# A two-layer float32 decoder trunk: streaming the high and low halves of the activations as one 512-column product

## The chip, the cores and the metric

The kernel runs on one core of one Trainium2 chip. The metric is the device time of one execution in microseconds, as the median over repeated runs of the same program; lower is better. Besides these times there is one execution that was recorded by the hardware profiler, and every row shown below comes from that execution. Engines are named as the profile names them: PE is the matrix engine, PEld its weight loads, DVE the vector engine, ACT the scalar engine, POOL the GpSimd engine, SP the queue that issues the loads.

## The reference, cut to what matters

Two layers (`DEPTH = 2`) over 256 positions and a width of 1024. Each layer computes

```python
h = rmsnorm(x, norm1[l]); proj = h @ w_in[l]
hq, hf, hi, hg, aq, ak, av, ga, gb = split_cols(proj)
...                                   # gated recurrence on hq, hf, hi, hg -> y_a
...                                   # sliding-window attention on aq, ak, av -> y_b
x = x + (sigmoid(ga) * y_a + sigmoid(gb) * y_b) @ w_o[l]
h2 = rmsnorm(x, norm2[l])
x = x + (silu(h2 @ w_gate[l]) * (h2 @ w_up[l])) @ w_down[l]
```

and a final rmsnorm follows. All of it is float32. The hidden width of the feed-forward part is 2816, that is 22 blocks of 128.

## The kernel before

**Products in three terms.** A float32 product is made from three products in the faster type `float32r`: each operand is split into a high half (the value rounded to `float32r`) and a low half (what the rounding left), and high·high, high·low and low·high are added up in PSUM; low·low is left out. Weights are split as they arrive: ACT casts a *unit* of 128 x 1024 weights to its high half `wh`, and DVE subtracts to get the low half `wl` (`ahead`, lines 192 to 203). There are 300 units. A unit waits for one of five buffers (`NW = 5`), which comes free when PE has used the unit that was in it; the raw weights lie in three buffers of 1 MB (`NRAW = 3`) that SP fills. `take(n)` (line 205) hands out the next units and asks for the following ones; `used()` (line 211) counts a finished unit and asks for the unit four further on.

**Activations.** `Norm` (line 272) transposes x, multiplies it by the gain and splits it into the two tiles `xh` and `xl`, each [128, 8, 256]: eight blocks `k` of the width by 256 positions. There is one buffer of each.

**Two forms of the product.** In `form_a` (line 222) the activations are the stationary operand and 512 columns of weights stream: each product is 128 x 512. It serves most projections, and `down` (line 848) does the same with `mm3`. In `form_b` (line 249) a 128 x 128 block of weights is the stationary operand and the 256 positions stream, so that the result comes out transposed. One unit is eight values of `k` with three products of 256 columns each, 24 in all, into half of a PSUM bank (a bank holds 512 float32 values per partition). `form_b` serves

- the 16 units of hf and hq per layer (`pb`, lines 713 to 721), while the generator of the attention is advanced beside them,
- the 22 units of the gate (`pg`) and the 22 of the up projection (`pu`) per layer, in `gate_up` (line 812), which takes two units of each at a time: eleven calls per layer, sorted into six groups (the last of one call).

In `gate_up`, DVE multiplies the whole bank `pg` by the row factors `rb2` into `z`, ACT takes the sigmoid into `sgm`, DVE multiplies the two, then multiplies `z` by the bank `pu`; `split` (line 259) makes the halves `ah` and `al`. `down` uses them one group later: group `gi - 1` follows the `gate_up` calls of group `gi`, and after the last group the last two are done together.

**PSUM.** There are eight banks: four with the tag `mm`, which turn over among all projections, two `at` and two `hg`. During the feed-forward part `at` and `hg` hold the four sums of `down` (`acc`).

**Order.** Generators are advanced by `run` (line 352): at each `yield` of the main line of products, the side generators (attention, recurrence, norms) may issue their next piece. A scheduler then orders the instructions of each engine by this order and by when they are ready by its own reckoning; each engine executes its own list strictly in order.

Of the kernel before, what the change touches and what calls it, by code (L numbers as in the profile page):

```python
# [8 lines left out]
F32R = mybir.dt.float32r  # L9
# [3 lines left out]
ALU = mybir.AluOpType  # L13
AX = mybir.AxisListType

P = 128
D = 1024
S = 256
NT = S // P
DEPTH = 2  # L20
KT = D // P
# [19 lines left out]
def trunk(ctx, tc, x, norm1, w_in, lb_logits, hg_norm, attn_sinks, w_pa, w_pb, w_o, norm2,  # L41
# [4 lines left out]
    class Ordered:  # L46
        def __init__(self, engine):
            self.engine = engine
            self.always = engine is nc.tensor
# [10 lines left out]
    V, A, G, T = (Ordered(e) for e in (nc.vector, nc.scalar, nc.gpsimd, nc.tensor))  # L60

    hp = ctx.enter_context(tc.tile_pool(name="hp", bufs=1))
    hp.tile([P, 224], F32, tag="lead", name="lead")
    hp.tile([P, KT, S], F32R, tag="xh", name="xh_lead")
    hp.tile([P, KT, S], F32R, tag="xl", name="xl_lead")
    st = hp.tile([P, 8, P], F32, tag="st", name="st")
    cp = ctx.enter_context(tc.tile_pool(name="cp", bufs=1))
    rawp = ctx.enter_context(tc.tile_pool(name="rawp", bufs=NRAW))
# [5 lines left out]
    def psum(name, tag="mm"):  # L74
        return pp.tile([P, 512], F32, tag=tag, name=name, bufs=4 if tag == "mm" else 2)

    def btile(shape, name, tag="b", dt=F32):
        return big.tile(shape, dt, tag=tag, name=name, bufs=6)

    def ztile(shape, name, tag="z", dt=F32):  # L80
        return sm.tile(shape, dt, tag=tag, name=name, bufs={"z": 4, "hx": 4, "rp": 2}[tag])
# [110 lines left out]
    def ahead(n):  # L192
        while len(ready) < min(n, 2 * len(plan)):
            while loaded[0] < len(plan) and len(raws) < len(ready) + 4:
                load(loaded[0])
                loaded[0] += 1
            i = len(ready)
            shape = list(raws[i].shape)
            hi = wp.tile(shape, F32R, tag="wh", name=f"wh{i}")
            lo = wp.tile(shape, F32R, tag="wl", name=f"wl{i}")  # L200
            A.copy(hi, raws[i])
            V.tensor_tensor(lo, raws[i], hi.bitcast(F32), ALU.subtract)
            ready.append((hi, lo))

    def take(n):
        i = taken[0]
        ahead(i + max(n, NW - 1))
        taken[0] += n
        return ready[i:i + n]

    def used():
        done[0] += 1
        ahead(done[0] + NW - 1)
# [32 lines left out]
                    used()  # L246
                yield

    def form_b(ps, act, unit, ks=range(KT)):
        wh, wl = unit  # L250
        for k in ks:
            (ah, al), kk = act(k)
            T.matmul(ps, wh[:, k, :], ah[:, kk, :], start=k == 0, stop=False)
            T.matmul(ps, wh[:, k, :], al[:, kk, :], start=False, stop=False)
            T.matmul(ps, wl[:, k, :], ah[:, kk, :], start=False, stop=k == KT - 1)
            if k % 4 == 3:
                yield

    def split(hi, lo, src):
        A.copy(hi, src)  # L260
        V.tensor_tensor(lo, src, hi.bitcast(F32), ALU.subtract)
# [10 lines left out]
    class Norm:  # L272
        def __init__(self, gain, name):
            self.gain, self.name = gain, name
            self.xh = hp.tile([P, KT, S], F32R, tag="xh", name=f"xh_{name}")
            self.xl = hp.tile([P, KT, S], F32R, tag="xl", name=f"xl_{name}")
            self.rb = sm.tile([P, 1, S], F32, tag="rb", name=f"rb_{name}", bufs=1)
            self.ss = sm.tile([P, NT, 3], F32, tag="ss", name=f"ss_{name}")
            self.r = [sm.tile([P, 1], F32, tag=f"r{t}", name=f"r_{name}{t}") for t in range(NT)]

        def act(self, k):
            return (self.xh, self.xl), k
# [53 lines left out]
    def start(gen, wait=0):  # L336
        sides.append([gen, wait])
        return sides[-1]
# [9 lines left out]
    def finish(side):  # L348
        while side[0] is not None:
            step(side)  # L350
# [8 lines left out]
    def layer(l, n1):  # L359
        act, rs, rb, spread = n1.act, n1.r, n1.wide(), n1.spread  # L360
# [327 lines left out]
        def recurrence():  # L688
            while atd[0] is not None:
                yield 1  # L690
            for g in range(2):
                decays(g)
            yield YD
            for g in range(2):
                yield from scores(g)
                yield 2
                yield from outputs(g)
# [15 lines left out]
        for g in range(2):  # L713
            for dst in fqk[g][:2]:
                for b in range(2):
                    ps = psum(f"pb{l}{g}{b}").rearrange("p (a c) -> p a c", a=2)
                    units = take(2)
                    for i in range(2):
                        yield from form_b(ps[:, i, :], act, units[i])
                        used()  # L720
                    V.tensor_tensor(dst[:, 2 * b:2 * b + 2], ps, rb, ALU.mult)
        rec = start(recurrence(), 1)

        def put_gate(c):
# [59 lines left out]
        n2 = Norm(g2[:, l], f"n2_{l}")  # L784
# [21 lines left out]

        for p_ in parts:
            finish(p_)
        act2, rs2, rb2, spread2 = n2.act, n2.r, n2.wide(), n2.spread
        acc = [[psum(f"acc{l}{t}{c}", "at" if t == 0 else "hg") for c in range(2)] for t in range(NT)]  # L810

        def gate_up(gi, b, ah, al):
            first = gi == 0 and b == 0
            pg = psum(f"pg{l}{gi}{b}").rearrange("p (a c) -> p a c", a=2)
            pu = psum(f"pu{l}{gi}{b}").rearrange("p (a c) -> p a c", a=2)
            z = ztile([P, 2, S], f"zg{l}{gi}{b}")
            sgm = ztile([P, 2, S], f"sgm{l}{gi}{b}")

            def mid():
                V.tensor_tensor(z, pg, rb2, ALU.mult)  # L820
                A.activation(sgm, z, AF.Sigmoid)
                V.tensor_tensor(z, z, sgm, ALU.mult)

            units = take(4)
            if first:
                for ks in (range(KT // 2), range(KT // 2, KT)):
                    yield from form_b(pg[:, 0, :], act2, units[0], ks)
                    yield from form_b(pu[:, 0, :], act2, units[2], ks)
                spread2()
                yield from form_b(pg[:, 1, :], act2, units[1])  # L830
                mid()
                used()
                used()
                yield from form_b(pu[:, 1, :], act2, units[3])
                used()
                used()
            else:
                for i in range(2):
                    yield from form_b(pg[:, i, :], act2, units[i])
                    used()  # L840
                mid()
                for i in range(2):
                    yield from form_b(pu[:, i, :], act2, units[2 + i])
                    used()
            V.tensor_tensor(z, pu, z, ALU.mult)
            split(ah[:, 2 * b:2 * b + 2], al[:, 2 * b:2 * b + 2], z)

        def down(item, ts_, c, units, tell):
# [14 lines left out]
        for gi, (b0, nb) in enumerate(groups):  # L863
            ah = btile([P, 4, S], f"ah{l}{gi}", "r", F32R)
            al = btile([P, 4, S], f"al{l}{gi}", "r", F32R)
            for b in range(nb // 2):
                yield from gate_up(gi, b, ah, al)
            pend.append((b0, nb, ah, al))
            if gi and gi < len(groups) - 1:
                item = pend.pop(0)  # L870
                for c in range(2):
                    yield from down(item, range(NT), c, take(2), True)
# [65 lines left out]
    for l in range(DEPTH):  # L938
        hold = []

        def whole():
            hold.append((yield from layer(l, nx)))

        run(whole())
        nx = hold[0]
# [53 lines left out]
```

## Time and profile before

| | |
|---|---|
| median of 3 runs | 957.61 us (957.34 to 957.65) |
| profiled execution, its own time | 957.52 us |
| span of that execution, first to last instruction | 955.8 us |
| mean granted clock of PE, as a share of full speed | 0.998 |
| instructions | 16173 |
| moved by DMA | 161.24 MB, mean 169 GB/s |

The span is what the rows can explain; 1.7 us of the profiled execution's own time lie around it. A group row gives the number of instructions, their summed busy time, the mean of one, and the idle time of the engine just ahead of them. The mean of one matmul runs from its start to its modelled end, and neighbours overlap: the distance between starts is shorter than that mean. The chain rows divide the time without overlap.

### The profile page before, as it was taken

What the parts mean: (1) busy time and instruction counts of PE and PEld (TensorE: products, weight loads), DVE (VectorE), ACT (ScalarE), POOL (GpSimd) and SP (SyncE); (2) the same over time, 40 slices, a digit from 0 to 9 for tenths busy, and PEclk for the clock granted to TensorE, in tenths of its full rate; (3) what the DMA queues carried; (4) which work ended last, traced back from release to release, by engine and by line L of the source; (5) the groups of instructions that cost most, each with busy time, mean ns of one, the idle gap of its engine ahead of it and who ended that gap; (6) DMA issues with size and microseconds to landing.
All of it is one profiled execution on the core that took longest, in us unless ns stands there. A gap on an engine that the chain in (4) does not pass through costs nothing.

```text
span 955.8 us, 16173 instructions
## 1 busy us (share of the span) xinstructions
PE 940.6 (98%) x6666; PEld 830.2 (87%) x6666; DVE 639.3 (67%) x1056; ACT 502.6 (53%) x794; POOL 16.4 (2%) x28
## 2 busy tenths in 40 slices
PE   7999999999999999999999999999999999999996
PEld 5879997878889999999878899878788899999995
DVE  6566769976677656555575676798857766556554
ACT  6555595545445444444365765855454544444442
POOL 1000000000000000000000000000000000000000
PEclk9999999999999999999999999999999999999999
DMA  8635444544445555555465334554545565555531
GB/s 283 225 129 172 148 157 140 170 135 173 149 162 180 186 203 182 176 184 195 151 207 190 132 133 138 172 178 133 161 159 180 162 197 177 177 190 190 193 133 44
DMA packets 110937, 161.24 MB, mean 169 GB/s; under 512 B 2768, under 2 KB 64400, under 8 KB 110864
## 3 DMA queue, kind: packets, MB, share of 16 engines
q1 hardware_dynamic: 110160, 159.12, 51.2%
q8 instruction: 52, 0.85, 0.4%
q10 hardware_dynamic: 704, 1.10, 0.3%
q14 instruction: 21, 0.17, 0.0%
HBM read 159.15 MB, written 1.05 MB: 168 GB/s over the span
## 4 chain that ended last, share of the span: by engine, by line
PE 96%; ACT 1%; DMA 1%; DVE 1%; issue 0%; POOL 0%; POOLq 0%; ACTq 0%
PE pg L55 13%; PE pu L55 13%; PE acc L55 12%; PE pb L55 10%; PE yb L55 5%; PE ga L55 5%; PE gb L55 5%; PE gate L55 5%; PE ya L55 5%; PE wo L55 5%; PE aq L55 5%; PE v L55 4%; PE akv L55 2%; PE qk L55 1%; PE pv L55 1%; PE o L55 1%
## 5 line engine op out<-in xcount | busy, mean ns | idle before, releaser
L55 ACT CAST wh<-raw 128x1024 fp32r<-128x1024 f32 x300 | 314.1, 1048 | 356.8 <-PE pg L55 71.8
L55 DVE TENSOR_TENSOR wl<-raw,wh 128x1024 fp32r<-128x1024 f32 x300 | 366.4, 1224 | 198.5 <-ACT wh L55 196.3
L55 PE MATMUL pg<-xh_n,wh 128*128 128x256 f32 x352 | 99.9, 284 | 0.0
L55 PE MATMUL pu<-xh_n,wh 128*128 128x256 f32 x352 | 99.9, 284 | 0.0
L55 PE MATMUL pg<-xl_n,wh 128*128 128x256 f32 x352 | 99.8, 284 | 0.0
L55 PE MATMUL pu<-xl_n,wh 128*128 128x256 f32 x352 | 99.8, 283 | 0.0
L55 PE MATMUL pu<-xh_n,wl 128*128 128x256 f32 x352 | 99.8, 283 | 0.0
L55 PE MATMUL pg<-xh_n,wl 128*128 128x256 f32 x352 | 99.7, 283 | 0.0
L55 PE MATMUL pb<-xh_n,wh 128*128 128x256 f32 x256 | 74.5, 291 | 0.0
L55 PE MATMUL pb<-xh_n,wl 128*128 128x256 f32 x256 | 72.7, 284 | 0.0
L55 PE MATMUL pb<-xl_n,wh 128*128 128x256 f32 x256 | 72.5, 283 | 0.0
L55 PE MATMUL acc<-wl,ah 128*128 128x512 f32 x176 | 68.9, 392 | 0.0
L55 PE MATMUL acc<-wh,al 128*128 128x512 f32 x176 | 68.6, 390 | 0.0
L55 PE MATMUL acc<-wh,ah 128*128 128x512 f32 x176 | 68.4, 392 | 0.0
L55 PEld LDWEIGHTS pg<-xl_n,wh 128*128 128x128 f32 x352 | 67.6, 192 | 0.4
L55 PEld LDWEIGHTS pg<-xh_n,wh 128*128 128x128 f32 x352 | 67.6, 192 | 0.4
L55 PEld LDWEIGHTS pu<-xh_n,wl 128*128 128x128 f32 x352 | 67.7, 192 | 0.0
L55 PEld LDWEIGHTS pu<-xl_n,wh 128*128 128x128 f32 x352 | 67.7, 192 | 0.0
L55 PEld LDWEIGHTS pu<-xh_n,wh 128*128 128x128 f32 x352 | 67.6, 192 | 0.0
L55 PEld LDWEIGHTS pg<-xh_n,wl 128*128 128x128 f32 x352 | 67.6, 192 | 0.0
L55 PEld LDWEIGHTS pb<-xh_n,wh 128*128 128x128 f32 x256 | 49.1, 192 | 3.0 <-issue 3.0
L55 PEld LDWEIGHTS pb<-xl_n,wh 128*128 128x128 f32 x256 | 49.2, 192 | 0.0
(232 smaller groups left out, 1856.2 us busy)
## 6 DMA issues: line engine op xcount, KB each, us to landing
raw<-in_w_in SPq DMA_DIRECT2D x58, 1024.0 KB, 5.1
raw<-in_w_gate SPq DMA_DIRECT2D x22, 1024.0 KB, 5.2
raw<-in_w_up SPq DMA_DIRECT2D x22, 1024.0 KB, 5.2
raw<-in_w_down SPq DMA_DIRECT2D x22, 1024.0 KB, 5.0
raw<-in_w_pb SPq DMA_DIRECT2D x8, 1024.0 KB, 5.0
raw<-in_w_pa SPq DMA_DIRECT2D x8, 1024.0 KB, 5.2
raw<-in_w_o SPq DMA_DIRECT2D x8, 1024.0 KB, 5.0
raw<-in_w_in SPq DMA_DIRECT2D x4, 512.0 KB, 6.2
```

The costliest lines, as they stand in the source:

```text
L55: ins = call(*args, **kw)
```

## The change

`xh` and `xl` become the two halves of one tile `xx` of shape [128, 8, 2, 256], so that for each `k` the high and the low half lie side by side as 512 columns. `form_b` then makes one product of `wh` with all 512 columns and one of `wl` with the 256 high columns: two products for each `k` instead of three. The result fills a whole bank, with the part from the low halves in its right half. A new function `join` adds the two halves: ACT copies the right half to SBUF and DVE adds the left half to it. Every unit has a bank of its own, and the operations that read `pg`, `pu` and `pb` from PSUM read the joined values from SBUF. The diff, cut to its core:

```diff
-    hp.tile([P, KT, S], F32R, tag="xh", name="xh_lead")
-    hp.tile([P, KT, S], F32R, tag="xl", name="xl_lead")
+    hp.tile([P, KT, 2, S], F32R, tag="xx", name="xx_lead")
...
-    def form_b(ps, act, unit, ks=range(KT)):
+    def form_b(ps, n, unit, ks=range(KT)):
         wh, wl = unit
         for k in ks:
-            (ah, al), kk = act(k)
-            T.matmul(ps, wh[:, k, :], ah[:, kk, :], start=k == 0, stop=False)
-            T.matmul(ps, wh[:, k, :], al[:, kk, :], start=False, stop=False)
-            T.matmul(ps, wl[:, k, :], ah[:, kk, :], start=False, stop=k == KT - 1)
+            if k < KT - 1:
+                T.matmul(ps, wh[:, k, :], n.xx[:, k], start=k == 0, stop=False)
+            T.matmul(ps[:, 0:S], wl[:, k, :], n.xx[:, k, 0, :], start=False, stop=False)
+            if k == KT - 1:
+                T.matmul(ps, wh[:, k, :], n.xx[:, k], start=False, stop=True)
             if k % 4 == 3:
                 yield
+
+    def join(dst, ps):
+        A.copy(dst, ps[:, S:])
+        V.tensor_tensor(dst, ps[:, 0:S], dst, ALU.add)
...
-                    ps = psum(f"pb{l}{g}{b}").rearrange("p (a c) -> p a c", a=2)
                     units = take(2)
                     for i in range(2):
-                        yield from form_b(ps[:, i, :], act, units[i])
+                        ps = psum(f"pb{l}{g}{b}{i}")
+                        yield from form_b(ps, n1, units[i])
+                        join(dst[:, 2 * b + i], ps)
                         used()
-                    V.tensor_tensor(dst[:, 2 * b:2 * b + 2], ps, rb, ALU.mult)
+                    V.tensor_tensor(dst[:, 2 * b:2 * b + 2], dst[:, 2 * b:2 * b + 2], rb, ALU.mult)
...
-            pg = psum(f"pg{l}{gi}{b}").rearrange("p (a c) -> p a c", a=2)
-            pu = psum(f"pu{l}{gi}{b}").rearrange("p (a c) -> p a c", a=2)
+            pg = [psum(f"pg{l}{gi}{b}{i}") for i in range(2)]
+            pu = [psum(f"pu{l}{gi}{b}{i}") for i in range(2)]
...
-                V.tensor_tensor(z, pg, rb2, ALU.mult)
+                V.tensor_tensor(z, z, rb2, ALU.mult)
...
                 for i in range(2):
-                    yield from form_b(pg[:, i, :], act2, units[i])
+                    yield from form_b(pg[i], n2, units[i])
+                    join(z[:, i], pg[i])
                     used()
                 mid()
                 for i in range(2):
-                    yield from form_b(pu[:, i, :], act2, units[2 + i])
+                    yield from form_b(pu[i], n2, units[2 + i])
+                    join(sgm[:, i], pu[i])
                     used()
-            V.tensor_tensor(z, pu, z, ALU.mult)
+            V.tensor_tensor(z, z, sgm, ALU.mult)
```

The first call of `gate_up` in a layer, which works on two units in turn, is changed in the same way.

## Rows read from the trace of the kernel before

**Rows 1.** The page: busy time of the engines, and the last chain by engine

```profile
PE 940.6 (98%) x6666; PEld 830.2 (87%) x6666; DVE 639.3 (67%) x1056; ACT 502.6 (53%) x794; POOL 16.4 (2%) x28
...
PE 96%; ACT 1%; DMA 1%; DVE 1%; issue 0%; POOL 0%; POOLq 0%; ACTq 0%
```

**Rows 2.** The chain that ended last, in order of time: start us, us, what

```profile
94.64 5.95 PE pb L55 x48
...
146.54 11.15 PE gate L55 x48
...
200.89 5.49 PE yb L55 x24
...
338.27 10.91 PE acc L55 x48
349.18 5.75 PE pg L55 x48
354.93 5.76 PE pu L55 x48
360.69 5.76 PE pg L55 x48
```

**Rows 3.** Groups, shapes kept apart, PE: form B products, then one of 512 columns

```profile
L55 PE MATMUL pg<-xl_n,wh 128*128 128x256 f32 x352 | 99.8, 284 | 0.0
L55 PE MATMUL pu<-xl_n,wh 128*128 128x256 f32 x352 | 99.8, 283 | 0.0
...
L55 PE MATMUL pb<-xl_n,wh 128*128 128x256 f32 x256 | 72.5, 283 | 0.0
...
L55 PE MATMUL acc<-wh,al 128*128 128x512 f32 x176 | 68.6, 390 | 0.0
```

**Rows 4.** Groups, shapes kept apart, ACT and DVE

```profile
L55 ACT CAST wh<-raw 128x1024 fp32r<-128x1024 f32 x300 | 314.1, 1048 | 356.8 <-PE pg L55 71.8 <-PE acc L55 68.3 <-PE pu L55 63.4
...
L55 ACT COPY rb_n<-rp_n 128x256 f32<-128x256 f32 x4 | 1.5, 366 | 1.7 <-PE rp_n L55 1.7
...
L55 DVE TENSOR_TENSOR wl<-raw,wh 128x1024 fp32r<-128x1024 f32 x300 | 366.4, 1224 | 198.5 <-ACT wh L55 196.3
L55 DVE TENSOR_TENSOR zg<-pg,rb_n 128x512 f32<-128x512 f32 x22 | 15.2, 692 | 15.1 <-PE pg L55 15.1
L55 DVE TENSOR_TENSOR zg<-zg,sgm 128x512 f32<-128x512 f32 x22 | 15.1, 686 | 0.0
...
L55 DVE TENSOR_TENSOR att1l<-pv,att1h 128x256 fp32r<-128x256 f32 x8 | 3.1, 420 | 0.7 <-ACT att1h L55 0.7
```

**Rows 5.** Stretches: from:to and length, busy us and count per engine, PEclk, DMA share, GB/s

```profile
0.00:16.00 16.00, 9.31 (x33) 6.99 (x34) 8.40 (x13) 8.85 (x15) 2.62 (x11) 1.00 0.85 303
...
90.00:128.00 38.00, 38.00 (x331) 36.20 (x329) 25.87 (x77) 23.07 (x54) 0.00 (x0) 1.00 0.38 119
128.00:158.00 30.00, 30.00 (x168) 25.21 (x165) 24.60 (x31) 23.80 (x35) 0.00 (x0) 1.00 0.53 173
...
338.00:372.00 34.00, 34.00 (x243) 32.11 (x242) 19.88 (x20) 14.68 (x16) 0.00 (x0) 1.00 0.56 186
```

**Rows 6.** Timeline of ACT in one call of gate_up

```profile
351.97 1.05 ACT L55 CAST wh<-raw 128x1024 fp32r<-128x1024 f32 x1 [1.66 <-PE pg L55]
354.85 1.05 ACT L55 CAST wh<-raw 128x1024 fp32r<-128x1024 f32 x1 [1.83 <-PE pg L55]
```

**Rows 7.** Timeline of DVE in the first call of gate_up of layer 0

```profile
295.17 0.69 DVE L55 TENSOR_TENSOR xl_n<-xg_n,xh_n 128x512 fp32r<-128x512 f32 x1 [0.42 <-ACT xh_n L55]
```

**Rows 8.** Timeline at the end of layer 0: ACT, then DVE

```profile
470.81 1.06 ACT L55 CAST wh<-raw 128x1024 fp32r<-128x1024 f32 x1 [6.77 <-PE acc L55]
...
464.70 0.68 DVE L55 TENSOR_TENSOR al<-zg,ah 128x512 fp32r<-128x512 f32 x1
```

More of the change, by code (lines that the diff above doesn't have):

```diff
@@ L274, in __init__ @@
             self.gain, self.name = gain, name
-            self.xh = hp.tile([P, KT, S], F32R, tag="xh", name=f"xh_{name}")
-            self.xl = hp.tile([P, KT, S], F32R, tag="xl", name=f"xl_{name}")
+            self.xx = hp.tile([P, KT, 2, S], F32R, tag="xx", name=f"xx_{name}")
+            self.xh, self.xl = self.xx[:, :, 0, :], self.xx[:, :, 1, :]
             self.rb = sm.tile([P, 1, S], F32, tag="rb", name=f"rb_{name}", bufs=1)
@@ L808, in layer @@
             finish(p_)
-        act2, rs2, rb2, spread2 = n2.act, n2.r, n2.wide(), n2.spread
+        rs2, rb2, spread2 = n2.r, n2.wide(), n2.spread
         acc = [[psum(f"acc{l}{t}{c}", "at" if t == 0 else "hg") for c in range(2)] for t in range(NT)]
@@ L826, in gate_up @@
                 for ks in (range(KT // 2), range(KT // 2, KT)):
-                    yield from form_b(pg[:, 0, :], act2, units[0], ks)
-                    yield from form_b(pu[:, 0, :], act2, units[2], ks)
+                    yield from form_b(pg[0], n2, units[0], ks)
+                    yield from form_b(pu[0], n2, units[2], ks)
+                join(z[:, 0], pg[0])
                 spread2()
-                yield from form_b(pg[:, 1, :], act2, units[1])
+                yield from form_b(pg[1], n2, units[1])
+                join(z[:, 1], pg[1])
                 mid()
+                join(sgm[:, 0], pu[0])
                 used()
                 used()
-                yield from form_b(pu[:, 1, :], act2, units[3])
+                yield from form_b(pu[1], n2, units[3])
+                join(sgm[:, 1], pu[1])
                 used()
```

## The prediction

> **What bounds the kernel now.** I read the page first. PE is busy for 98% of the span, and the chain that ended last is PE for 96% of it [rows 1]; DVE (67%) and ACT (53%) have room. So a saving of PE time shows up in the time, and work added to DVE and ACT shows up only where PE then waits for it. The granted clock is 1.00, the 2.4 GHz level, in every stretch I looked at [rows 5], and nothing here gives PE a pause that would change it.
>
> The next question is what one product costs PE. The groups say 284 ns for 256 columns and 390 ns for 512 [rows 3]. Taken at their word, 960 replaced pairs (352 of pg, 352 of pu, 256 of pb) would save 2 x 284 - 390 = 178 ns each. But these means overlap: a start is not a whole mean after the one before. The chain in order of time divides the time without overlap, and there 48 products of 256 columns take 5.75 to 5.76 us, 120.0 ns each, and 48 of 512 columns take 10.91 us, 227.3 ns each [rows 2]. The 256 further columns cost 107.3 ns, 0.42 ns a column, which is one column per cycle at 2.4 GHz. What is left, 120.0 - 107.3 = 12.7 ns, is the fixed part of one product with its weight load. The reader should see here that the stream of columns is nearly everything: the change streams exactly as many columns as before (512 + 256 against 3 x 256 for each k) and saves one fixed part.
>
> **The change part by part.**
>
> *Products.* Each k goes from three products to two, from 3 x 120.0 = 360.0 ns to 227.3 + 120.0 = 347.3 ns. There are 960 values of k [rows 3], and all of them lie on the chain: 960 x 12.7 = 12.2 us. A unit goes from 24 x 120.0 = 2.88 us to 8 x 347.3 = 2.78 us. No row shows a 512-column product with this stationary operand, so I bound the price by other 512-column rows: 228.8 ns (24 of yb in 5.49 us) and 232.3 ns (48 of gate in 11.15 us, the beginning of a stage in it) [rows 2], which leave 11.2 and 7.7 ns per pair, 10.8 and 7.4 us. From above, if the whole fixed part of both products went, it would be 2 x 12.7 x 960 = 24 us, but the acc row still has a fixed part with 512 columns, so I keep 12.2. I take the acc row because it stands directly beside pg and pu and nothing is mixed into it.
>
> A rule speaks against this saving. The rows show a fixed part of 12.7 ns. The Trainium skill ("TensorE: Matmul & The Clock Gate", section "Back-to-back issue gap") gives N/2.4 + 2.5 ns for warm products, so a fixed part of only 2.5 ns; by that the sum would be about 2.4 us, an estimate from that page. The trace does not agree: 256 columns would then take 109 ns, and they take 120.0.
>
> *The joins.* Each of the 120 form B units (16 + 44 per layer) adds an ACT copy of 128 x 256 from PSUM, 0.37 us as rb_n, and a DVE addition of 128 x 256 with one operand in PSUM, 0.42 us as att1l [rows 4]. That is 44 us more on ACT and 50 us more on DVE. The multiplications by rb stay and read SBUF instead of PSUM: 0.69 us either way [rows 4], so no change. If all the joins stood on the path, it would be 120 x 0.79 = 95 us; if they are hidden, nothing. They are near nothing, for these reasons:
>
> - In a steady stretch of the feed-forward part DVE is busy 19.88 of 34 us and ACT 14.68 [rows 5]. A period holds eight form B units, so DVE goes to 23.2 and ACT to 17.6 of some 33.2 us, 70% and 53%.
> - PE does not read z, sgm or pu. The halves ah and al are read by down one group later, behind at least the next 10.91 us of acc. At the end of a layer al is ready at 465.4 us, and the last weights that the last down needs are only cast from 470.81 on [rows 8]: a join of 0.79 us fits in.
> - Queue order: the join's copy on ACT waits for the end of its unit, and behind it stands the cast of a coming unit. Casts now start at the end of a unit, when its buffer comes free [rows 6], and serve the unit five further on. Held up by one unit plus the copy, the halves are ready 0.37 + 1.05 + 1.22 = 2.6 us after a unit's end, with three units of 2.78 us, 8.3 us, to go. Slack 5.7 us. DVE's subtraction stands behind the addition in the same way.
> - PSUM: one call of gate_up now takes all four mm banks instead of two. A bank is cleared some 0.9 us after its unit and wanted again three units later, 8.3 us.
> - SP: nothing is moved past it. Its loads start when a cast and a subtraction free a raw buffer, so a little later in each round; the stretch moves 186 GB/s at a share of 0.56 where the opening stretch moved 303 [rows 5], so a rate higher by 1% is covered.
>
> *One tile for both halves.* A 512-column product needs the low half at once, where until now its high half could go first. This can matter only where PE stands right behind the split: the first gate_up of a layer, where xl takes 0.69 us after xh [rows 7]. Bound: 0 to 0.7 us in each of two layers. Since the first calls also hold k's and units that are ready earlier, I take 0.15 us each, 0.3 us in all. In the pb stretch and behind it, where ACT is busy 23.80 and DVE 24.60 of 30 us [rows 5], a late cast could cost something; the 5.7 us of slack cover it, and I put 0 there with up to 3 us kept for the range (about eight copies, 8 x 0.37 us, laid fully on the path).
>
> *Sum.* 957.52 - 12.2 + 0.3 = 945.6 us against the profiled execution. The median of the runs shown is 0.1 us higher, so 945.7.
>
> **The rivals.**
>
> *The fixed part is smaller than it looks (no change).* If most of the 12.7 ns belonged to the conditions of the 256-column stages and came back with 512 columns and these weights, say as in a row at 237.5 ns, the pair would give 2.5 ns: 2.4 us, 955.2 us. Against it: four kinds of 512-column rows lie at 227 to 232 ns. The skill's rule above leads to about this time. Chance 0.05, and the losses of the next rival, if they ate most of the gain, lead there too, 0.03.
>
> *Part of the gain is given back.* The added 94 us on ACT and DVE reorder their lists; around the end of pb both are near full [rows 5], and side work of the attention and the recurrence shares them. Three to eight microseconds of PE waits would leave 949 to 953.5. For: 48 products of pb already take 5.95 instead of 5.76 us [rows 2], so that stage is less smooth. Against: PE has no idle time there now. Chance 0.14.
>
> *Slower: PE waits for PSUM banks.* With all four mm banks in one call of gate_up, the next unit's first product must wait for the join if the banks do not turn over in time. It decides from the point where a bank is wanted before its DVE addition is done. The price is up to copy plus addition, 0.79 us a unit, 95 us, 1040 us; the kernel comes out slower by over 0.2% once a unit loses (12.2 + 1.9)/120 = 0.12 us. For: half as many blocks fit into the banks as before. Against: three other units lie between. Chance 0.05.
>
> *The means of the groups are right after all.* 960 x 178 ns = 171 us, 787 us. Against it: 24 products at 284 ns would take 6.8 us a unit and two units take 5.76. Also smaller windfalls, down to twice the fixed part (24 us, 933 us), go here. Chance 0.03.
>
> **How the numbers follow.** The forecast, 945.7 us, has a chance of 0.70, from 943.5 (fixed parts a little larger, nothing lost) to 948.9 (the gate row's price of a product, and some loss). The range has to hold 8 in 10, so it goes on into the rival of the given-back gain up to 951. A measurement of this kernel can tell about 0.2%, 1.9 us, from no change. Faster: 0.70 + 0.14 + 0.03 and about half of the 0.08 of the first rival, since 955.2 lies just beyond the limit, 0.91; within 0.2%: 0.04; slower: 0.05.
>
> **What would show it.** In the changed profile: 960 fewer PE instructions (6666 to 5706) and as many fewer weight loads; in the chain in order of time, two form B units in about 5.56 us, so a gate-and-up call of 11.1 us against 11.5; acc unchanged at 10.91 us for 48. ACT about 547 us busy and DVE about 690. Casts that still wait for PE, not PE for casts. Wrong would be: pairs of a 512- and a 256-column product that take 355 ns or more (the fixed part), products that wait for a DVE addition (banks), or idle time of PE behind ACT's casts.

## The result, and the profile after

The changed kernel takes 951.12 us (median, 950.94 to 951.57) against 957.61 us: a ratio of 0.9934 with a 95% interval of 0.9916 to 0.9951. The sign and the bounding engine came out as forecast, the size did not: 6.5 us were saved where 11.9 were expected, and the time lies 0.1 us above the range.

The page of the changed kernel shows what the change was meant to do, beside [rows 1]:

```profile
span 949.5 us, 14350 instructions
...
PE 934.3 (98%) x5706; PEld 778.0 (82%) x5706; DVE 678.5 (71%) x1176; ACT 538.4 (57%) x914; POOL 16.5 (2%) x28
...
PE 95%; DVE 2%; ACT 2%; DMA 0%; issue 0%; POOL 0%; POOLq 0%; ACTq 0%; SPq 0%
```

There are 960 products and 960 weight loads fewer, and 120 instructions more on each of DVE and ACT. PE is still what ends last. The chain in order of time (start us, us, what), which answers to [rows 2], shows where the gain stayed small:

```profile
336.81 10.88 PE acc L55 x48
347.69 5.63 PE pg L55 x32
353.33 5.64 PE pu L55 x32
358.97 5.64 PE pg L55 x32
```

Two units take 5.64 us, not the 5.56 us forecast: 5.64 us / 16 = 352.5 ns for each k instead of 347.3. The acc stage beside it has not become dearer (10.88 us for 48, 226.7 ns each). PE's timeline (start us, us, engine, line, operation) shows that nothing is waited for; the products simply stand further apart than in the stages that the price came from:

```profile
348.22 0.40 PE L55 MATMUL pg<-xx_n,wh 128*128 128x512 f32 x1
348.46 0.28 PE L55 MATMUL pg<-xx_n,wl 128*128 128x256 f32 x1
348.58 0.40 PE L55 MATMUL pg<-xx_n,wh 128*128 128x512 f32 x1
348.82 0.28 PE L55 MATMUL pg<-xx_n,wl 128*128 128x256 f32 x1
348.93 0.40 PE L55 MATMUL pg<-xx_n,wh 128*128 128x512 f32 x1
```

Read the starts, not the lengths: from a 512-column product to the next start it is 0.24 us, where acc has 0.227; from a 256-column one 0.12 and 0.11. Over the whole gate-and-up part the mean distance is 235.1 ns after a 512-column product (700 of them) and 117.7 ns after one of 256 (704). All means of this kind below are worked out from the starts in the record of the same part, leaving out distances over 260 ns, which stand beside other products (the transposes and the attention's) or hold a wait.

The joins are where they were expected to be. Groups of the changed kernel, which answer to [rows 4]:

```profile
L55 ACT COPY zg<-pg 128x256 f32<-128x256 f32 x44 | 16.4, 373 | 57.2 <-PE pg L55 57.2
...
L55 DVE TENSOR_TENSOR zg<-pg,zg 128x256 f32<-128x256 f32 x44 | 18.7, 424 | 23.0 <-ACT zg L55 22.9
L55 DVE TENSOR_TENSOR sgm<-pu,sgm 128x256 f32<-128x256 f32 x44 | 18.4, 421 | 11.1 <-ACT sgm L55 11.1
```

0.37 us on ACT and 0.42 us on DVE, as taken from rb_n and att1l; over all four kinds (zg, sgm, q, f) the copies add up to 43.9 us and the additions to 50.4, as forecast. That the page has ACT at 538.4 and DVE at 678.5 us, not at the 547 and 690 forecast, is because neighbouring records overlap, and the page counts the time that two of them share once: DVE's single durations add up to 742.8 us, 48.7 more than before. And a stretch of the feed-forward part, columns as in [rows 5]:

```profile
338.00:372.00 34.00, 34.00 (x180) 29.09 (x179) 23.24 (x30) 17.58 (x26) 0.00 (x0) 1.00 0.60 188
```

DVE 23.24 and ACT 17.58 of 34 us (forecast 23.2 and 17.6), PE without a pause, its granted clock at 1.00.

### The profile page after: what moved, and what is told of

The parts are those of the page before. It is cut to its first block, busy times and chain, and to the rows that moved or that the text cites. A ratio compares the mean times of both kernels' runs of the same rounds, so it can differ in the third digit from the quotient of the medians.

```text
span 949.5 us, 14350 instructions
## 1 busy us (share of the span) xinstructions
PE 934.3 (98%) x5706; PEld 778.0 (82%) x5706; DVE 678.5 (71%) x1176; ACT 538.4 (57%) x914; POOL 16.5 (2%) x28
## 4 chain that ended last, share of the span: by engine, by line
PE 95%; DVE 2%; ACT 2%; DMA 0%; issue 0%; POOL 0%; POOLq 0%; ACTq 0%; SPq 0%
PE pg L55 13%; PE pu L55 13%; PE acc L55 12%; PE pb L55 9%; PE yb L55 5%; PE ga L55 5%; PE gb L55 5%; PE gate L55 5%; PE wo L55 5%; PE ya L55 5%; PE aq L55 5%; PE v L55 4%; PE akv L55 2%; PE qk L55 1%; PE o L55 1%; PE pv L55 1%
## 5 line engine op out<-in xcount | busy, mean ns | idle before, releaser
L55 PE MATMUL pu<-xx_n,wh 128*128 128x512 f32 x352 | 125.1, 398 | 0.0
L55 PE MATMUL pg<-xx_n,wh 128*128 128x512 f32 x352 | 125.0, 398 | 0.0
L55 PE MATMUL pu<-xx_n,wl 128*128 128x256 f32 x352 | 91.8, 281 | 0.0
L55 PE MATMUL pg<-xx_n,wl 128*128 128x256 f32 x352 | 91.6, 281 | 0.0
L55 PE MATMUL pb<-xx_n,wh 128*128 128x512 f32 x256 | 91.3, 403 | 0.0
L55 PEld LDWEIGHTS pg<-xx_n,wh 128*128 128x128 f32 x352 | 64.8, 188 | 12.4
L55 PEld LDWEIGHTS pu<-xx_n,wh 128*128 128x128 f32 x352 | 64.8, 188 | 11.9
L55 PEld LDWEIGHTS pu<-xx_n,wl 128*128 128x128 f32 x352 | 66.5, 189 | 4.0
L55 PEld LDWEIGHTS pg<-xx_n,wl 128*128 128x128 f32 x352 | 66.5, 189 | 4.0
L55 PE MATMUL pb<-xx_n,wl 128*128 128x256 f32 x256 | 66.9, 281 | 0.0
```

The costliest lines, as they stand in the source:

```text
L55: ins = call(*args, **kw)
```

## The experiments

The first theory (A) was that right after a change of size PE's products stand further apart and come back only after some ten of the same size, as the starts of the acc stage suggest. Its rivals: (B) the joins slow PE, (C) a 512-column stream of these activations is slower by itself.

**Eight of one size in a row.** The products of the changed kernel in another order:

```diff
-        for k in ks:
-            if k < KT - 1:
-                T.matmul(ps, wh[:, k, :], n.xx[:, k], start=k == 0, stop=False)
-            T.matmul(ps[:, 0:S], wl[:, k, :], n.xx[:, k, 0, :], start=False, stop=False)
...
+        if ks[0] == 0:
+            T.matmul(ps, wh[:, 0, :], n.xx[:, 0], start=True, stop=False)
+        for k in ks:
+            T.matmul(ps[:, 0:S], wl[:, k, :], n.xx[:, k, 0, :], start=False, stop=False)
+        if len(ks) == KT:
+            yield
+        for k in ks:
+            if k:
+                T.matmul(ps, wh[:, k, :], n.xx[:, k], start=False, stop=k == KT - 1)
+        yield
```

The last unit's seven and the next unit's first 512-column product make eight.

> Only the order of the products in a form B unit changes: runs of eight of one size (eight 512-column products, then eight of 256) instead of alternating sizes. Theory A (settling: right after a change of size a 512-column product starts 230 to 241 ns before the next, and comes down to 227 ns after some ten of the same size; alternating sizes never settle): eight 512-column products at 234, 233, 231, 232, 228, 229, 230, 227 ns and eight of 256 at 113, 119 and six of 120 make 2.80 us a unit, two units 5.59 us instead of 5.64; the time falls by 120 x 0.024 = 2.9 us to about 948.2 us. Theory B (the joins' copies and additions slow PE) and theory C (a 512-column stream of these activations is slower by itself): the order changes nothing, 5.64 us for two units, 951 us.

Measured: 948.42 us (ratio to the kernel before 0.9907, 0.9893 to 0.9920). Chain and timeline of this kernel:

```profile
380.63 5.59 PE pg L55 x32
...
387.23 2.00 PE L55 MATMUL pu<-xx_n,wh 128*128 128x512 f32 x8
389.07 1.12 PE L55 MATMUL pu<-xx_n,wl 128*128 128x256 f32 x8
```

Eight of 512 columns run from 387.23 to 389.07, 230 ns each. In the full runs of eight (72 and 82 of them) the mean distances by place are 233.6, 235.7, 228.4, 232.4, 230.8 and three times 226.7 ns; for 256 columns 113.4, 119.2 and then 120.0: the first product of 256 columns behind 512 comes sooner, the first five of 512 later. The same products and joins in another order are 2.7 us faster: the order of sizes counts, which B and C do not explain.

**One size only.** `ps[:, 0:S]` and `n.xx[:, k, 0, :]` become `ps` and `n.xx[:, k]` in the product of `wl`, so that the low-low term is computed as well.

> The low half of the weights streams both halves of the activations too, so that every product of a form B unit has 512 columns (it adds the low-low term, 256 more columns for each k). Theory A: no change of size inside the stage, so each product takes 227 ns, 16 of them 3.63 us a unit, 7.26 us for two units; 960 x (453.8 - 352.5 ns) = 97 us more, 1048 us. Theory C: each takes some 232 to 235 ns, 7.4 to 7.5 us for two units, 1059 to 1064 us. Theory B: PE is disturbed as before by the joins, so irregular distances between starts remain, above 7.3 us for two units.

Measured: 1048.58 us (ratio 1.0951, 1.0936 to 1.0966). Its chain:

```profile
341.10 7.25 PE pu L55 x32
348.36 7.25 PE pg L55 x32
```

32 products in 7.25 us are 226.6 ns each, at 1400 distances 226.9 ns on average, with the joins running beside them. This ends C, and B as a cause of the wider distances; it also shows that the change of weights from `wh` to `wl` at every product is harmless.

**The joins with three products of 256 columns.** For k = 1 to 6:

```diff
-                T.matmul(ps, wh[:, k, :], n.xx[:, k], start=k == 0, stop=False)
+                T.matmul(ps[:, 0:S], wh[:, k, :], low, start=False, stop=False)
+                T.matmul(ps[:, S:], wh[:, k, :], n.xx[:, k, 1, :], start=False, stop=False)
```

> The joins and banks of the changed kernel with the products of the one before: six of the eight k of a unit take three 256-column products (the low half of the activations into the right half of the bank), the first and last k stay fused. Theory A: the six k cost 360 ns each as in the kernel before, with starts 120.0 ns apart, the two fused ones some 353; 720 x 7 ns = 5 us more than the changed kernel, about 956 us. Theory B (the joins cost some 5 us): they do so here too, so 240 x 12.7 ns of saving against 5 us of joins, about 959.5 us, and starts 120 ns apart are broken up wherever a join runs. Theory C: 957.6 - 240 x 7.5 ns = 955.8 us, as A.

Measured: 955.27 us (ratio 0.9977, 0.9968 to 0.9986), as A and C had it and 4 us below B. Inside the long runs of 256 columns, from about the tenth product on, the starts are 120.0 ns apart again.

**No joins.** DVE reads only the left halves, with `rb` and with `z`; the low halves of the activations are left out of the result, the products stay.

```diff
-                        join(dst[:, 2 * b + i], ps)
+                        V.tensor_tensor(dst[:, 2 * b + i], ps[:, 0:S], rb[:, 0, :], ALU.mult)
```

> The products of the changed kernel without its joins: the right half of each bank (the low half of the activations) is left unread, and DVE reads the left half from PSUM, so that 120 copies on ACT and 120 additions on DVE are gone. Theory A and theory C: PE keeps its 352.5 ns for each k, two units 5.64 us, and the time stays within 0.7 us of 951.1. Theory B: PE's distances fall to 347 ns for each k, and the time to about 946 us.

Measured: 950.19 us (ratio 0.9923, 0.9911 to 0.9936), 0.9 us below the changed kernel; two units still take 5.64 us. So the joins cost 0.9 us in all, none of it in the products. Some 0.4 us of it has a place: the attention beside `pb` in layer 0. The chain of the changed kernel:

```profile
82.82 1.23 DVE wl L55
84.05 0.94 DVE f L55 x2
84.99 2.27 DVE wl L55 x2
87.25 0.34 DVE att0l L55
87.60 0.04 issue
87.64 1.10 PE qp L55 x8
```

and the kernel without joins in the same place:

```profile
84.69 1.50 PE pv L55 x16
86.19 0.55 PE pb L55 x2
86.74 0.44 PE qp L55 x4
87.18 0.23 PE pb L55
87.41 0.44 PE qp L55 x4
```

In the first, DVE is full from 82.82 on (`DVE f` holds an addition of a join), att0l comes late, and the transposes `qp` wait for it, and PE stands still. The list of waits of the changed kernel (who for whom: us in total, times, longest) has it too:

```profile
PE qp L55 <- DVE att0l L55: 0.3, 1, 0.3
```

By the distance of the starts (548 ns from 87.09 to 87.64, where some 118 are usual) it is 0.43 us. Without the joins they do not wait. The rest is in small pieces: the distances from one product to the next start of PE are longer with the joins than without behind rp_n (by 0.20 us), yb (0.15), ga (0.12) and acc (0.11), and so is the time behind the last product (0.16), each too little to be told from noise by itself. Behind pg, pu and pb together the distances add up to 7.2 us less than before, with the joins and without them.

**Sixteen of one size, and two.** Two units together in two banks, with `form_pair` in place of two calls of `form_b`:

```diff
+        for i in range(2):
+            for k in range(KT - 1):
+                high(i, k)
+            yield
+        for i in range(2):
+            for k in range(KT):
+                T.matmul(pss[i][:, 0:S], units[i][1][:, k, :], n.xx[:, k, 0, :], start=False, stop=False)
...
+        for i in range(2):
+            high(i, KT - 1)
+        yield
```

`high(i, k)` is the 512-column product of unit i. For runs of two, in `form_b`:

```diff
...
+            T.matmul(ps[:, 0:S], wl[:, k, :], n.xx[:, k, 0, :], start=False, stop=False)
+            if k % 2:
+                high(k)
+                if k < KT - 1:
+                    high(k + 1)
```

Left out at the top is the 512-column product of k = 0, which comes first.

> Two units are worked on together in two banks: sixteen 512-column products in a row, then sixteen of 256 (in the first feed-forward call of a layer runs of eight at most). Settling (theory A, with the distances measured in e1_grouped): 233.7, 235.3, 228.6, 232.0, 230.7 and eleven of 226.7 ns make 228.4 ns on average, with 119.8 for the 256-column ones 348.2 ns for each k against 349.9 in e1_grouped; two units 5.57 us; some 1.3 us less than e1_grouped, about 947.1 us, if the two weight units that are held twice as long are not waited for. If a change of size has a fixed price: two units 5.56 us, about 946.6 us, not to be told apart here. A wait for weights would show as idle time of PE ahead of a unit.

> Runs of two products of one size (two of 512 columns, two of 256, and so on): half as many changes of size as in the changed kernel. Settling (theory A): the first and the second 512-column product after a change both still take 234 to 235 ns and the 256-column ones 117 to 120, so 353 ns for each k as when alternating, two units 5.64 us, 951 us. Rival (each change of size has a fixed price, (352.5 - 347.3)/2 = 2.6 ns): half the changes, 349.9 ns for each k, two units 5.60 us, about 948.6 us.

Measured: 946.60 us for runs of sixteen (ratio 0.9885, 0.9869 to 0.9902) and 948.27 us for runs of two (0.9903, 0.9888 to 0.9917). Chains, sixteen and then two:

```profile
412.68 5.55 PE pg L55 x32
418.24 5.57 PE pu L55 x32
```

```profile
413.79 5.57 PE pg L55 x32
419.36 5.57 PE pu L55 x32
```

Sixteen came out as theory A had it (a fixed price per change had said 946.6 us, so this run does not tell the two apart) and is the fastest kernel of this study, 4.5 us below the changed one. Of these, (352.8 - 348.7) x 960 = 3.9 us are the distances; about 0.4 us more is the wait of qp for att0l, which the list of waits of this kernel does not have. Two units are held at a time, and PE is not seen waiting for their weights in the list of waits. Runs of two went against theory A, which had expected no gain from them: 233.1 and 116.1 ns, 349.2 for each k. They fit a fixed price of 2.6 ns per change of size. But that rival fails in runs of eight, where a fixed price would leave 347.3 + 5.2/8 = 348 ns for each k, 5.57 us, and 5.59 were measured. A price by place in the run fails too: eight's first places would make 233.6 + 113.4 = 347.0 ns for each k when alternating, where 352.8 were measured. So neither holds; what a product costs depends on more of what ran before it.

**Is it the place in PSUM, or the shortness of 256 columns?** In the first kernel the product of `wl` goes into `ps[:, S:]` instead of `ps[:, 0:S]`, which the join adds just the same. In the second it streams 384 columns and so adds half of the low-low term.

> The 256-column products of the low weights are added into the right half of the bank instead of the left; the joins add both halves, so the sum is the same. Theory A (what counts is the order of sizes): nothing changes, 512-column products some 235 ns before the next, 256-column ones 117, two units 5.64 us, 951 us. Rival (a 512-column product is held up because its first columns are added to the places that the 256-column product has just written): the distance between the two writes of a place doubles, the 512-column products come down towards 227 ns, two units towards 5.56 us, 946 us.

> The low half of the weights streams 384 columns (the high half and half of the low half of the activations; it adds the low-low term for half of the positions), so that sizes of 512 and 384 alternate. On the line through 120.0 and 226.7 ns a 384-column product would take 173.3 ns settled. Theory A (any change of size unsettles): 226.7 + 173.3 + some 6 = 406 ns for each k, two units 6.50 us, 951.1 + 960 x 53.5 ns = 1002.5 us. Rival (only a 256-column product is so short that the next weight load is late): 400 ns for each k, two units 6.40 us, 996.7 us.

Measured: 951.12 us (ratio 0.9934, 0.9922 to 0.9947) and 1008.66 us (1.0534, 1.0518 to 1.0550). The place in the bank changes nothing (235.0 and 117.6 ns). With 384 columns, the chain:

```profile
406.42 6.61 PE pu L55 x32
413.03 6.61 PE pg L55 x32
```

413 ns for each k, where the settled prices would add up to 400 and theory A had said 406 (1002.5 us, 6 us too few): 233.7 ns after 512 columns, 178.8 after 384 (173.3 on the line). So the rival that only 256 columns are too few to hide a weight load does not hold as it was put: mixing sizes costs here too, and more. A product of 384 columns, at 173 to 179 ns, is still shorter than the 188 ns with which its weight loads are recorded, so the test does not clear the weight loads altogether.

The orders side by side (two units: two form B units in the chain; 512, other: mean distance to the next start in ns):

| order of sizes | 512 | other | per k | two units, us | median, us |
|---|---|---|---|---|---|
| three of 256 (before) | | 120.2 | 360.7 | 5.76 | 957.61 |
| alternating (the change) | 235.1 | 117.7 | 352.8 | 5.64 | 951.12 |
| runs of two | 233.1 | 116.1 | 349.2 | 5.57 | 948.27 |
| runs of eight | 230.2 | 119.7 | 349.9 | 5.59 | 948.42 |
| runs of sixteen | 228.5 | 120.2 | 348.7 | 5.57 | 946.60 |
| 512 only | 226.9 | | 453.8 | 7.25 | 1048.58 |
| 512 and 384 alternating | 233.7 | 178.8 | 412.5 | 6.61 | 1008.66 |

## Why the prediction was wrong

*What bounds the kernel: right.* PE, before and after. That the lengths of the groups overlap and must not be subtracted was right as well: the rival of 787 us was off by more than 160 us.

*Products, the term that failed.* "From 3 x 120.0 = 360.0 ns to 227.3 + 120.0 = 347.3 ns" put together two prices, each read in a stage of one size only. Side by side in one stage they do not hold: 352.5 ns, so 7.5 ns for each k instead of 12.7, 7.2 us instead of 12.2. The starts agree: added up over the whole trace, the distances from each product to the next start of PE are 2.85 us less than before behind pg, 2.47 behind pu and 1.84 behind pb. The 5.0 us between 12.2 and 7.2 are most of the 5.4 us that are missing. The experiments show it as the cause: with the same joins, one size alone gives the settled 226.9 ns (512 only), and another order of the very same products gives back 2.7 us (eight) and 4.5 us (sixteen, 3.9 of them by the distances). The clue stood in the rows of before: the gate row, 232.3 ns at the beginning of a stage, was taken only as a bound. PE's timeline of before shows what the row begins with:

```profile
146.47 0.51 PE L55 MATMUL gate<-wh,xh_n 128*128 128x512 f32 x1
146.81 0.40 PE L55 MATMUL gate<-wl,xh_n 128*128 128x512 f32 x1
147.05 0.40 PE L55 MATMUL gate<-wh,xl_n 128*128 128x512 f32 x1
```

One distance of 0.34 us, then ten that average 233 ns, then 227. Those ten said that 512 columns cost more at the beginning of a stage. That the row's mean leaves 7.7 ns, almost the 7.5 measured, is luck: the new stage has 235.1 and 117.7 ns, not 232.3 and 120.0.

*The joins: nearly right.* Forecast as hidden, they cost 0.9 us by the kernel without them. Of the queues that were named, ACT's casts kept their slack (PE's list of waits names no cast for pb, pg or pu); it was DVE, behind whose full list the attention's att0l came late in layer 0. 7.2 - 0.9 = 6.3 us leaves 0.2 us of the 6.5 measured, within what the runs scatter. The step that lets a join fit in at the end of a layer did not quite hold: the weight loads of the last `down` now wait for `al` once in each layer, which the list of before does not have.

```profile
PEld acc L55 <- DVE al L55: 0.6, 2, 0.3
```

The kernel without joins has the same line, so it does not come from the joins alone, and all distances behind acc together are only 0.2 us longer than before.

*The first gate_up of a layer, the PSUM banks, SP: right.* PE's list of waits names neither pg nor pu nor pb, so no wait for a DVE addition or for a split half stands there. The rival that PE waits for banks did not come; 951 us in place of 945.7 is what the rival of the given-back gain gave as a time, but for another reason than its own: the products lost most of it, side work little.

*The range.* The case "gate row's price of a product, and some loss" was put at 948.9 us, while the text's own numbers give 957.52 - 7.4 = 950.1 before any loss. With the 3 us that the text keeps for losses it would have reached 953.1, past the 951.12 measured.

*The rule.* A fixed part of 13.3 ns is what runs of one size show: 512 columns alone take 226.7 ns, 256 alone 120.0, so 106.7 ns for 256 columns. The rival that most of the fixed part comes back (955.2 us) was closer in kind than I allowed: 5.2 of the 12.7 ns did come back in the new stage. The Trainium skill ("TensorE: Matmul & The Clock Gate", section "Back-to-back issue gap") has a fixed part of 2.5 ns, for what it calls an isolated product. No run here agrees with it for these products with a weight load each.

## What to carry to other kernels

Take the price of an instruction from a stage with the same neighbours, not only from one with the same shape; where no such stage exists, read the first products of a stage after a change of shape one by one, as a warning that the settled price may not be reached. When a sum is made from products of two sizes, order them in runs: here that was worth 2.7 to 4.5 us without a new wait in PE's list, and more than a third of what the fusion itself had brought.

## What the runs showed that I had not expected

Mixing sizes on PE widens the distance between products without any wait that a profile row names: 235.1 ns for a 512-column product in alternation with 256, against 226.7 settled, while the 256-column ones come a little sooner (117.7 against 120.0). In runs of eight and sixteen the first five 512-column products behind 256 columns stand 228 to 236 ns apart, and only the sixth is back at 226.7. How long this lasts depends on what ran before: acc's first six stand at 234.0, 235.5, 228.9, 232.4, 230.4 and 227.4 ns in the kernel before, behind three products of 256 for each k, but at 233.1 and then 227 to 228 in the changed one, behind the alternating stage. It is not the place written in PSUM (951.12 us with the other half of the bank), not the change of weights (226.9 ns with `wh` and `wl` in turn), and not 256 columns alone (413 ns with 384 instead of 400). Every product here has a weight load of its own, so no run separates the change of size from the load beside it. What in PE makes it so stays open: runs of two (349.2 ns for each k) are as good as runs of eight (349.9), and no simple price per change or per place in a run fits both.
